# Hybrid trunk: attention with its tokens in their own order, V made with tokens stationary

## The chip, the cores and the metric

The kernel runs on one core of a Trainium2 chip. The core has a matrix engine (TensorE, "PE" in the profile, with its weight loads shown apart as "PEld"), a vector engine (VectorE, "DVE"), a scalar engine (ScalarE, "ACT"), a general engine (GpSimd, "POOL") and an engine that issues DMAs (SyncE, "SP"). Working memory is SBUF, 128 partitions wide; matrix products land in PSUM, which has eight banks of 512 fp32 values per partition. The metric is the device time of one execution in microseconds, the median of several runs.

## The reference

Two residual layers over 512 tokens of 1024 features, in fp32. Layer 0 mixes tokens by causal pooling, layer 1 by attention; each is followed by a SwiGLU, and a last norm ends it. The change lies in layer 1's attention. Its 16 heads of 64 features fall into three groups: 6 heads look at a window of 128 consecutive tokens, 5 at every fourth token (window 512, dilation 4), 5 at every sixteenth (window 2048, dilation 16). Here they are called near heads (0 to 5) and far heads (6 to 15).

```python
ATTN_PATTERNS = ((128, 1), (512, 4), (2048, 16))     # HEAD_GROUPS = (6, 5, 5)

def attn_mixer(h, w_qkv, w_out):
    qkv = jnp.einsum('bsd,de->bse', h, w_qkv).reshape(B, S, 3, N_HEADS, HEAD_DIM)
    q = rope(qkv[:, :, 0]) * HEAD_DIM ** -0.5
    k = rope(qkv[:, :, 1])
    v = qkv[:, :, 2]
    ...
    for (window, dilation), n_g in zip(ATTN_PATTERNS, HEAD_GROUPS):
        o_g, lse_g = dilated_window_attention(q[:, :, sl], k[:, :, sl], v[:, :, sl], window, dilation)
        outs.append(o_g)
        lses.append(jax.nn.logsumexp(lse_g, axis=-1) - math.log(n_g))
    alpha = jax.nn.softmax(jnp.stack(lses, axis=-1), axis=-1)
    merged = jnp.concatenate(
        [o_g * (N_ATTN_GROUPS * alpha[:, :, g]).astype(o_g.dtype)[:, :, None, None] for g, o_g in enumerate(outs)],
        axis=2,
    ).reshape(B, S, D_ATTN)
    return jnp.einsum('bse,ed->bsd', merged, w_out)
```

Within `dilated_window_attention` the tokens of one residue (position modulo the dilation) see only each other, causally, up to the window.

## The kernel before

**Products in three terms.** Every large fp32 product is made of three in a rounded format (fp32r): an operand is split into `hi`, a rounded copy (a ScalarE copy), and `lo`, the rest (a VectorE subtraction), and the products hi x hi, hi x lo and lo x hi are added up in PSUM. `split` does so for activations (L311 to L313), `weights` for weights (L137, L138).

**Weights.** `enqueue` lists all weight tiles in the order of use. `weights(i)` (L119) issues the DMAs of the next tiles on SP's queue into a ring of five raw tiles, splits the next few, and hands out tile i. All engines but PE get their order from a scheduler that works from priorities; `tc.high_priority(URGENT)` raises the priority of what stands in it. PE's order is that of the program (`manual_schedule`).

**The normed input.** `h_hi` and `h_lo` hold the normed activations with features on partitions, 8 chunks of 512 tokens. `turned` (L329) fills them: it transposes a block of 128 tokens by PE and splits the result into its places, which `in_order` (L315) or `by_residue` (L319) gives. For attention it is `by_residue`: position r * 128 + j holds token 4 j + r, so that the tokens of one residue modulo 4 are consecutive. The tables of cosines and sines stand in the same order (`TOKENS`, L53).

**Queries and keys.** For each pair of heads t = 0 to 7, `project` (L226) makes q and k as 24 matmuls (8 chunks x 3 terms) with a 128 x 128 weight stationary and 512 tokens moving, and `rope` (L816) turns them: a shuffle and two multiplications (one on GpSimd), then an addition that writes the result. Its addition (L824 to L830) writes far heads' q and k as they stand; near heads' q into token order, and near heads' k into an order by block of 128 tokens, and by residue within it. The masks of the near heads (`key` in `_constants`, L1138) follow that order. The first three products are made in two halves of tokens (`by_halves`), because the last block of tokens comes late.

**Steps.** A counter of steps runs through this: `later(step)` (L922) runs one head's transposes and one set of scores that are due. `near_scores` and `far_scores` make the scores on PE, mask them and take the maxima on VectorE, and take exponentials on ScalarE (`soften`); `transposes` turns the exponentials by PE into `pT` one step later. `between(step)` (L1032) also starts the sums of the groups' shares at step 19, the groups' weights at 21, and their spread over the features, with a transposition on PE, at 22.

**V.** `v` holds tokens on partitions, four blocks of 128, for all 1024 features. Near heads' 384 features (`VA`) are made as three products with weights stationary and 512 tokens moving, steps 16 to 18; ScalarE copies each out in blocks (L1057), and `turn` (L1044) transposes its four blocks by PE (L1048) and copies them to `v` (L1049). The far heads' 640 features are made in two parts of 320 (`VB`): tokens are stationary, 128 of one residue at a time, the weights' 320 columns move, and four PSUM banks hold the four blocks through 4 x 2 chunks of features (L1071 to L1073), in steps 19 to 26. At the last chunk each block's bank is copied to `v`, two by ScalarE (L1078) and two by VectorE (L1076).

**The merge.** For each pair of heads, products of `v` and `pT` (L1100 to L1104) go to one PSUM bank of the same ring of four, VectorE multiplies by the shares (L1108), and the result is split into `h_hi`, `h_lo` for the output projection.

Of the kernel before, what the change touches and what calls it, by code (L numbers as in the profile page):

```python
# [17 lines left out]
P = 128  # L18
S = 512
# [30 lines left out]
)  # L50

TWO = [(g, i) for g in (0, 1) for i in (0, 3)] + [(g, i) for i in (1, 2, 4, 5, 6) for g in (0, 1)]
TOKENS = np.arange(S).reshape(J, R).T.reshape(-1)  # L53
BY_GROUP = [6, 7, 4, 5, 2, 3, 0, 1]


# [1 line left out]
def trunk_kernel(ctx: ExitStack, tc: tile.TileContext, x_in, xT, gam, gains, consts, ident_d, w0, wT, w1, wv, w_down, out):  # L58
# [260 lines left out]
    def by_residue(b):  # L319

        n = P // R

        def places(h, half, tp):
            at = h[:, 4 * half : 4 * half + 4, :].rearrange("p c (r j) -> p c r j", r=R)
            return at[:, :, :, b * n : (b + 1) * n], tp.rearrange("p c (i r) -> p c r i", r=R)

        return places

    def turned(norm, shift, b, tps, order):  # L329

# [183 lines left out]
    def ffn(layer, norm, third, nxt):  # L514
# [8 lines left out]
        with ExitStack() as fctx:  # L523
# [267 lines left out]
    with ExitStack() as actx:  # L791
# [17 lines left out]
        ap.tile([P, 8], F32, name="gap3")  # L809
        state = {}  # L810

        def blocks_of(a):

            return a.rearrange("p (r b i) -> p b r i", r=R, b=4)

        def rope(ps, t, name):  # L816
            a = aw.tile([P, S], F32, name="ropea")
            sw = aw.tile([P, S], F32, name="ropeb")
            nc.vector.stream_shuffle(sw, ps, PARTNER)
            nc.vector.tensor_mul(a, ps, cosr)  # L820
            nc.gpsimd.tensor_mul(sw, sw, sinr)
            out = aw.tile([P, S], F32, name=name, bufs=3)

            if t >= 3:  # L824
                nc.vector.tensor_add(out, a, sw)
            elif name == "k":
                nc.vector.tensor_add(out.rearrange("p (b r i) -> p b r i", b=4, r=R), blocks_of(a), blocks_of(sw))
            else:
                by_r = lambda z: z.rearrange("p (r j) -> p r j", r=R)
                nc.vector.tensor_add(out.rearrange("p (j r) -> p r j", r=R), by_r(a), by_r(sw))  # L830
            return out

        def slot(h, i):
# [94 lines left out]
                pend_tr.extend((step + 1, *got) for got in run(*args))  # L928

        h_hi, h_lo = tokens_at(0)  # L930
        late = lambda b: turned(norm, 0, b, [ptr.tile([P, 4, P], F32, name="tp") for _ in range(2)], by_residue(b))

        def by_halves(js):

            n = J // 2
            part = lambda z, i: z.rearrange("p (r j) -> p r j", r=R)[:, :, i * n : (i + 1) * n]
            got = [(mm.tile([P, S], F32, name="mm"), weights(j, held=i)) for i, j in enumerate(js)]
            for i in range(2):
                for at, (ps, (whi, wlo)) in enumerate(got):
                    if i == 0 and at == 2:  # L940
                        late(3)
                    for c in range(NC):
                        mm3(part(ps, i), whi[:, c, :], wlo[:, c, :], part(h_hi[:, c, :], i), part(h_lo[:, c, :], i),
                            i + c == 0, c == NC - 1, skip_group_check=True)
            return [ps for ps, _ in got]

# [92 lines left out]
                spread_weights()  # L1039


        to_turn = []

        def turn():  # L1044
            m, vt = to_turn.pop(0)
            tp = ptr.tile([P, 4, P], F32, name="tp")
            for b in range(4):
                nc.tensor.transpose(tp[:, b, :], vt[:, b * P : (b + 1) * P], ident)  # L1048
            nc.scalar.copy(v[:, :, m * P : (m + 1) * P], tp)  # L1049

        step = 16
        for m in range(3):
            ps = project(j_v0[m], h_hi, h_lo)
            if to_turn:
                turn()
            vt = aw.tile([P, S], F32, name="ropea")
            nc.scalar.copy(vt.rearrange("p (b r i) -> p b r i", b=4, r=R), blocks_of(ps))  # L1057
            to_turn.append((m, vt))
            between(step)
            step += 1  # L1060
        for part in range(2):
            at = VA + part * VB
            pv = [mm.tile([P, S], F32, name="mm") for _ in range(4)]
            for c in range(4):
                whi, wlo = weights(j_v[part][c])
                for b in range(4):
                    for kk in range(2):
                        kc = 2 * c + kk
                        o = pv[b][:, :VB]
                        xh, xl = (z[:, kc, b * P : (b + 1) * P] for z in (h_hi, h_lo))  # L1070
                        nc.tensor.matmul(o, lhsT=xh, rhs=whi[:, kk, :], start=kc == 0, stop=False)  # L1071
                        nc.tensor.matmul(o, lhsT=xh, rhs=wlo[:, kk, :], start=False, stop=False)
                        nc.tensor.matmul(o, lhsT=xl, rhs=whi[:, kk, :], start=False, stop=kc == NC - 1)  # L1073
                    if c == 3:
                        if b // 2:
                            nc.vector.tensor_copy(v[:, b, at : at + VB], pv[b][:, :VB])  # L1076
                        else:
                            nc.scalar.copy(v[:, b, at : at + VB], pv[b][:, :VB])  # L1078
# [12 lines left out]
        for t in range(8):  # L1091
            ps = mm.tile([P, S], F32, name="mm")
            for h in (2 * t, 2 * t + 1):
                base = HD * (h % 2)
                rows = slice(base, base + HD)
                cols = slice(h * HD, (h + 1) * HD)
                for b in range(4):
                    o = ps[rows, b * P : (b + 1) * P]
                    if h >= 6:
                        nc.tensor.matmul(o, lhsT=v[:, b, cols], rhs=pT[:, slot(h, b), :], start=True, stop=True)  # L1100
                    else:
                        nc.tensor.matmul(o, lhsT=v[:, b, cols], rhs=pT[:, slot(h, 2 * b), :], start=True, stop=b == 0)
# [3 lines left out]
            by_r = lambda z: z.rearrange("p (r j) -> p r j", r=R)  # L1106
            in_turn = lambda z: z.rearrange("p (j r) -> p r j", r=R)
# [13 lines left out]
def _constants():  # L1121
# [12 lines left out]
    cos = np.tile(np.concatenate([cos, cos], 0)[ROPE_ORDER], (2, 1))[:, TOKENS]  # L1134
    sin = np.tile(np.concatenate([-sin, sin], 0)[ROPE_ORDER], (2, 1))[:, TOKENS]
    q = np.arange(P)[:, None]
    k = np.arange(P)[None, :]
    key = R * (k % 32) + k // 32  # L1138
    near = np.where(key <= q, 0.0, NEG)
    prev = np.where(key >= q, 0.0, NEG)  # L1140
    own = np.where(k <= q, 0.0, NEG)
    comb = np.where((k <= q) & (k % 4 == q % 4), 0.0, NEG)
    parts = bands + [cos, sin, near, prev, near, own, comb]
    return np.ascontiguousarray(np.concatenate(parts, 1).astype(np.float32))


def _tiles(w, n):

    k = w.shape[0] // P
    return w.reshape(k, P, n, P).transpose(2, 1, 0, 3).reshape(n, P, k * P)  # L1150


def _layout(x, norm_mix, norm_ffn, norm_final, pool_w_in, pool_w_group, pool_scale, pool_w_out,
# [9 lines left out]
    w0 = np.concatenate([w_in, grp, qk, _tiles(qkv[:, 2 * D :], 8)[:3]], 0)  # L1163
    gu = [np.stack([_tiles(ffn_w_gate[i], NF), _tiles(ffn_w_up[i], NF)], 1).reshape(2 * NF, P, 1024) for i in range(2)]
    wv = qkv[:, 2 * D :].reshape(NC, P, D).transpose(1, 0, 2)
    wv = np.concatenate([wv[:, :, a:b].reshape(P, -1) for a, b in ((VA, VA + VB), (VA + VB, D))], 1)
# [19 lines left out]
```

## Time and profile before

| what | value |
|---|---|
| median of 3 runs | 1008.01 us (1007.27 to 1009.94) |
| the profiled execution | 1007.57 us |
| its span, first to last instruction | 1005.8 us |
| mean granted TensorE clock | 0.998 |
| near V, weights stationary, and the last scores | 557.9 to about 577.8 us of the span |
| far V, tokens stationary | about 577.8 to 607.5 us |
| merge of heads | about 607.5 to 622 us |

In a row of the timeline, the first number is the start in us from the span's start, the second the duration of the group, then engine, source line, operation, the tiles written and read, and the shapes; "x4" is a count, and a bracket at the end tells how long the engine had been idle and what released it. In a row of a line (`L830 DVE ...`) stand count, then shortest, median and longest duration in ns. In a row of groups, the numbers behind the bar are busy us in total and mean ns of one, then the idle time of the engine before them. In the table of stretches each engine has its busy us with the number of instructions. Matmuls are pipelined: one's duration includes time in which the next already runs.

### The profile page before, as it was taken

To read this page: it belongs to the slowest core of one execution; us is meant where nothing else is said; L and a number is where in the kernel's file an instruction comes from. 1 tells how busy PE (TensorE), PEld (TensorE's weight loads), DVE (VectorE), ACT (ScalarE), POOL (GpSimd) and SP (SyncE) were. 2 spreads that over 40 slices of the span, in tenths; PEclk is the share of its full clock that TensorE was granted. 3 is DMA by queue.
4 is the path that set the end of the run, shared out by engine and by line. 5 is a ranking of instruction groups with operands and counts; after the bars stand their busy time and mean duration, and the time that the engine had idled before them with its cause. 6 is when DMAs were issued, how large, how long until landed. Compare 5 with 4: busy or idle time off the path is not lost.

```text
span 1005.8 us, 16546 instructions
## 1 busy us (share of the span) xinstructions
PE 994.0 (99%) x6559; PEld 906.4 (90%) x6559; DVE 784.4 (78%) x1117; ACT 528.7 (53%) x834; POOL 110.8 (11%) x110
## 2 busy tenths in 40 slices
PE   9999999999999999999999999999999999999997
PEld 7888999989989998988788898889998998999895
DVE  6484899898897888787887557479989889788875
ACT  5573666545544554572454444357654554555354
POOL 0002010111002010002112032101011110111000
PEclk9999999999999999999999999999999999999999
DMA  9457276678559765523221249426766855975512
GB/s 353 155 189 167 63 210 158 158 199 236 144 129 288 169 150 144 188 83 99 71 69 53 82 152 268 85 63 186 183 155 193 235 147 123 290 178 141 153 64 83
DMA packets 76189, 157.30 MB, mean 156 GB/s; under 512 B 5760, under 2 KB 5888, under 8 KB 76112
## 3 DMA queue, kind: packets, MB, share of 16 engines
q1 hardware_dynamic: 57856, 121.00, 35.7%
q0 software_dynamic: 17968, 34.99, 20.3%
q8 instruction: 51, 0.84, 0.3%
q14 instruction: 26, 0.21, 0.1%
q10 hardware_dynamic: 288, 0.27, 0.1%
HBM read 154.08 MB, written 2.13 MB: 155 GB/s over the span
## 4 chain that ended last, share of the span: by engine, by line
PE 94%; DVE 2%; DMA 1%; ACT 1%; issue 1%; ACTq 0%; DVEq 0%
PE p L602 25%; PE r L602 13%; PE r L685 10%; PE mm L602 6%; PE p L685 5%; PE mm L222 4%; PE mm L224 4%; PE mm L223 4%; PE mm L739 3%; PE mm L685 2%; PE mm L354 2%; PE mm L352 2%; PE mm L353 2%; DMA wraw<-wT 1%; PE early L223 1%; PE early L224 1%
## 5 line engine op out<-in xcount | busy, mean ns | idle before, releaser
L137 ACT CAST whi<-wraw 128x1024 fp32r<-128x1024 f32 (+2 forms) x190 | 185.4, 978 | 178.4 <-issue 34.4
L138 DVE TENSOR_TENSOR wlo<-wraw,whi 128x1024 fp32r<-128x1024 f32 (+2 forms) x190 | 220.4, 1160 | 74.9 <-ACT whi L137 74.1
L137 ACT CAST whi<-vraw 128x1024 fp32r<-128x1024 f32 (+1 forms) x102 | 99.6, 976 | 144.8 <-DVE vraw L140 54.0
L602 PE MATMUL p<-t_hi,wlo 128*128 128x256 f32 x528 | 149.8, 284 | 0.0
L602 PE MATMUL p<-t_lo,whi 128*128 128x256 f32 x528 | 149.5, 283 | 0.0
L602 PE MATMUL p<-t_hi,whi 128*128 128x256 f32 x528 | 148.4, 281 | 0.0
L138 DVE TENSOR_TENSOR wlo<-vraw,whi 128x1024 fp32r<-128x1024 f32 (+1 forms) x102 | 114.9, 1127 | 14.2 <-ACT whi L137 13.9
L602 PEld LDWEIGHTS p<-t_hi,whi 128*128 128x128 f32 x528 | 100.0, 189 | 0.0
L602 PE MATMUL r<-h_hi,wlo 128*128 128x256 f32 x352 | 99.9, 284 | 0.0
L602 PEld LDWEIGHTS p<-t_hi,wlo 128*128 128x128 f32 x528 | 99.6, 189 | 0.0
L602 PE MATMUL r<-h_lo,whi 128*128 128x256 f32 x352 | 99.6, 283 | 0.0
L602 PEld LDWEIGHTS p<-t_lo,whi 128*128 128x128 f32 x528 | 99.3, 188 | 0.0
L602 PE MATMUL r<-h_hi,whi 128*128 128x256 f32 x352 | 99.0, 281 | 0.0
L140 DVE TENSOR_TENSOR vraw<-vraw,wraw 128x1024 f32<-128x1024 f32 x68 | 76.6, 1127 | 0.8
L106 POOL DMA_DIRECT2D wraw<-w x22 | 26.6, 1211 | 428.0 <-DMA wraw<-w 171.2
L602 PEld LDWEIGHTS r<-h_hi,whi 128*128 128x128 f32 x352 | 66.7, 189 | 0.0
L602 PEld LDWEIGHTS r<-h_hi,wlo 128*128 128x128 f32 x352 | 66.4, 189 | 0.0
L602 PEld LDWEIGHTS r<-h_lo,whi 128*128 128x128 f32 x352 | 66.2, 188 | 0.0
L222 PE MATMUL mm<-h_hi,whi 128*128 128x512 f32 (+1 forms) x176 | 65.2, 370 | 0.0
L224 PE MATMUL mm<-h_hi,wlo 128*128 128x512 f32 (+1 forms) x176 | 63.6, 361 | 0.0
L223 PE MATMUL mm<-h_lo,whi 128*128 128x512 f32 (+1 forms) x176 | 63.5, 361 | 0.0
L685 PE MATMUL r<-whi,u_lo 128*128 128x512 f32 x144 | 56.1, 390 | 0.0
(315 smaller groups left out, 2489.9 us busy)
## 6 DMA issues: line engine op xcount, KB each, us to landing
wraw<-w SPq DMA_DIRECT2D x116, 512.0 KB, 4.8
wraw<-w_down SPq DMA_DIRECT2D x32, 512.0 KB, 3.6
vraw<-w SPq DMA_DIRECT2D x22, 512.0 KB, 5.2
wraw<-w POOLq DMA_DIRECT2D x22, 512.0 KB, 7.6
vraw<-w POOLq DMA_DIRECT2D x22, 512.0 KB, 8.4
wraw<-wT SPq DMA_DIRECT2D x16, 512.0 KB, 4.7
wraw<-w_down SPq DMA_DIRECT2D x24, 256.0 KB, 2.7
vraw<-w_down SPq DMA_DIRECT2D x6, 512.0 KB, 5.3
```

Source lines behind the costliest of these rows:

```text
L106: nc.gpsimd.dma_start(dst, more, accum_op=ALU.add)
L137: nc.scalar.copy(hi[:, :n], raw[:, :n])
L138: nc.vector.tensor_sub(lo[:, :n], raw[:, :n], hi[:, :n].bitcast(F32))
L140: nc.vector.tensor_add(raws[into][:, :n], raws[into][:, :n], raws[more][:, :n])
L222: nc.tensor.matmul(ps, lhsT=whi, rhs=xhi, start=first, stop=False, **kw)
L223: nc.tensor.matmul(ps, lhsT=whi, rhs=xlo, start=False, stop=False, **kw)
L224: nc.tensor.matmul(ps, lhsT=wlo, rhs=xhi, start=False, stop=last, **kw)
L352: nc.tensor.matmul(ps, lhsT=xhi, rhs=w[0][:, k, :], start=first, stop=False)
L353: nc.tensor.matmul(ps, lhsT=xhi, rhs=w[1][:, k, :], start=False, stop=False)
L602: nc.tensor.matmul(ps[:, g, :], lhsT=w[:, g, c, :], rhs=xx[:, c, :], start=i in (0, 1, 3) and g + c + k == 0, stop=c == 3 and k == 2, skip ...
L685: nc.tensor.matmul(acc[t], lhsT=u, rhs=w, start=i in (0, 1, 3) and c + k == 0, stop=c == len(pairs) - 1 and k == 2, skip_group_check=True,)
L739: nc.tensor.matmul(ps, lhsT=u, rhs=w[:, m, :], start=z + m + k == 0, stop=z == 1 and m == 1 and k == 2,)
```

## The change

The normed input of attention stays in token order, and so do the tables of angles. Near heads' q and k are written as they stand; far heads' q and k are written by residue by the addition in `rope`, which reads its two operands at a step of four tokens. All of V is made with tokens stationary, in three parts of 384, 320 and 320 features: in the first a block is 128 consecutive tokens, in the others it is every fourth token of the 512, so that the weight load of the far parts reads the tokens of `h_hi` and `h_lo` at a step of four. The products of near V with weights stationary, their copies and transposes go. The evictions of all parts stand in `tc.high_priority(URGENT)`. There are 12 steps of V instead of 11, four for each part; the step numbers in `between` stay. Near masks become plain causal ones.

```diff
-VA = 6 * HD
-VB = 5 * HD
+V_PARTS = ((0, 6 * HD), (6 * HD, 5 * HD), (11 * HD, 5 * HD))
...
-    j_v0 = [enqueue(w0[26 + i], (8, P)) for i in range(3)]
-    j_v = []
-    for at in (0, VB):
-        j_v.append([enqueue(wv[:, 8 * at + c * 2 * VB : 8 * at + (c + 1) * 2 * VB], (2, VB)) for c in range(4)])
+    j_v = [[enqueue(wv[:, 8 * at + c * 2 * n : 8 * at + (c + 1) * 2 * n], (2, n)) for c in range(4)] for at, n in V_PARTS]
...
-            turn_block = lambda b: turned(norm, 0, b, [r_tile() for _ in range(2)], by_residue(b))
+            turn_block = lambda b: turned(norm, 0, b, [r_tile() for _ in range(2)], in_order(b))
...
+        by_r = lambda z: z.rearrange("p (r j) -> p r j", r=R)
+        in_turn = lambda z: z.rearrange("p (j r) -> p r j", r=R)
...
-            if t >= 3:
+            if t < 3:
                 nc.vector.tensor_add(out, a, sw)
-            elif name == "k":
-                nc.vector.tensor_add(out.rearrange("p (b r i) -> p b r i", b=4, r=R), blocks_of(a), blocks_of(sw))
             else:
-                by_r = lambda z: z.rearrange("p (r j) -> p r j", r=R)
-                nc.vector.tensor_add(out.rearrange("p (j r) -> p r j", r=R), by_r(a), by_r(sw))
+                nc.vector.tensor_add(by_r(out), in_turn(a), in_turn(sw))
...
-        late = lambda b: turned(norm, 0, b, [ptr.tile([P, 4, P], F32, name="tp") for _ in range(2)], by_residue(b))
+        late = lambda b: turned(norm, 0, b, [ptr.tile([P, 4, P], F32, name="tp") for _ in range(2)], in_order(b))
...
-                        mm3(part(ps, i), whi[:, c, :], wlo[:, c, :], part(h_hi[:, c, :], i), part(h_lo[:, c, :], i),
+                        mm3(ps[:, HALVES[i]], whi[:, c, :], wlo[:, c, :], h_hi[:, c, HALVES[i]], h_lo[:, c, HALVES[i]],
...
-        to_turn = []
-
-        def turn():
...
         step = 16
-        for m in range(3):
-            ps = project(j_v0[m], h_hi, h_lo)
-            if to_turn:
-                turn()
-            vt = aw.tile([P, S], F32, name="ropea")
-            nc.scalar.copy(vt.rearrange("p (b r i) -> p b r i", b=4, r=R), blocks_of(ps))
-            to_turn.append((m, vt))
-            between(step)
-            step += 1
-        for part in range(2):
-            at = VA + part * VB
+        for part, (at, n) in enumerate(V_PARTS):
+            tokens = lambda z, b: z[:, b * P : (b + 1) * P] if part == 0 else in_turn(z)[:, b, :]
             pv = [mm.tile([P, S], F32, name="mm") for _ in range(4)]
             for c in range(4):
                 whi, wlo = weights(j_v[part][c])
                 for b in range(4):
                     for kk in range(2):
                         kc = 2 * c + kk
-                        o = pv[b][:, :VB]
-                        xh, xl = (z[:, kc, b * P : (b + 1) * P] for z in (h_hi, h_lo))
+                        o = pv[b][:, :n]
+                        xh, xl = (tokens(z[:, kc, :], b) for z in (h_hi, h_lo))
                         nc.tensor.matmul(o, lhsT=xh, rhs=whi[:, kk, :], start=kc == 0, stop=False)
                         nc.tensor.matmul(o, lhsT=xh, rhs=wlo[:, kk, :], start=False, stop=False)
                         nc.tensor.matmul(o, lhsT=xl, rhs=whi[:, kk, :], start=False, stop=kc == NC - 1)
                     if c == 3:
-                        if b // 2:
-                            nc.vector.tensor_copy(v[:, b, at : at + VB], pv[b][:, :VB])
-                        else:
-                            nc.scalar.copy(v[:, b, at : at + VB], pv[b][:, :VB])
-                if to_turn:
-                    turn()
+                        with tc.high_priority(URGENT):
+                            if b // 2:
+                                nc.vector.tensor_copy(v[:, b, at : at + n], pv[b][:, :n])
+                            else:
+                                nc.scalar.copy(v[:, b, at : at + n], pv[b][:, :n])
                 between(step)
                 step += 1
...
-    key = R * (k % 32) + k // 32
-    near = np.where(key <= q, 0.0, NEG)
-    prev = np.where(key >= q, 0.0, NEG)
     own = np.where(k <= q, 0.0, NEG)
+    prev = np.where(k >= q, 0.0, NEG)
     comb = np.where((k <= q) & (k % 4 == q % 4), 0.0, NEG)
-    parts = bands + [cos, sin, near, prev, near, own, comb]
+    parts = bands + [cos, sin, own, prev, own, own, comb]
```

More of the change, by code (lines that the diff above doesn't have):

```diff
@@ L52 @@
 TWO = [(g, i) for g in (0, 1) for i in (0, 3)] + [(g, i) for i in (1, 2, 4, 5, 6) for g in (0, 1)]
-TOKENS = np.arange(S).reshape(J, R).T.reshape(-1)
 BY_GROUP = [6, 7, 4, 5, 2, 3, 0, 1]
@@ L317, in in_order @@
         return lambda h, half, tp: (h[:, 4 * half : 4 * half + 4, b * P : (b + 1) * P], tp)
[L319 to L327, printed above, removed]
     def turned(norm, shift, b, tps, order):
@@ L810, in trunk_kernel @@
         state = {}
-        def blocks_of(a):
-            return a.rearrange("p (r b i) -> p b r i", r=R, b=4)
+        by_r = lambda z: z.rearrange("p (r j) -> p r j", r=R)
+        in_turn = lambda z: z.rearrange("p (j r) -> p r j", r=R)
         def rope(ps, t, name):
@@ L930, in trunk_kernel @@
         h_hi, h_lo = tokens_at(0)
-        late = lambda b: turned(norm, 0, b, [ptr.tile([P, 4, P], F32, name="tp") for _ in range(2)], by_residue(b))
+        late = lambda b: turned(norm, 0, b, [ptr.tile([P, 4, P], F32, name="tp") for _ in range(2)], in_order(b))
         def by_halves(js):
-            n = J // 2
-            part = lambda z, i: z.rearrange("p (r j) -> p r j", r=R)[:, :, i * n : (i + 1) * n]
             got = [(mm.tile([P, S], F32, name="mm"), weights(j, held=i)) for i, j in enumerate(js)]
@@ L1039, in between @@
                 spread_weights()
-        to_turn = []
-        def turn():
[L1045 to L1049, printed above, removed]
-        step = 16
-        for m in range(3):
-            ps = project(j_v0[m], h_hi, h_lo)
-            if to_turn:
-                turn()
-            vt = aw.tile([P, S], F32, name="ropea")
-            nc.scalar.copy(vt.rearrange("p (b r i) -> p b r i", b=4, r=R), blocks_of(ps))
-            to_turn.append((m, vt))
-            between(step)
-            step += 1
-        for part in range(2):
-            at = VA + part * VB
+        step = 16
+        for part, (at, n) in enumerate(V_PARTS):
+            tokens = lambda z, b: z[:, b * P : (b + 1) * P] if part == 0 else in_turn(z)[:, b, :]
             pv = [mm.tile([P, S], F32, name="mm") for _ in range(4)]
@@ L1133, in _constants @@
     sin = np.sin(ang.astype(np.float64))
-    cos = np.tile(np.concatenate([cos, cos], 0)[ROPE_ORDER], (2, 1))[:, TOKENS]
-    sin = np.tile(np.concatenate([-sin, sin], 0)[ROPE_ORDER], (2, 1))[:, TOKENS]
+    cos = np.tile(np.concatenate([cos, cos], 0)[ROPE_ORDER], (2, 1))
+    sin = np.tile(np.concatenate([-sin, sin], 0)[ROPE_ORDER], (2, 1))
     q = np.arange(P)[:, None]
     k = np.arange(P)[None, :]
-    key = R * (k % 32) + k // 32
-    near = np.where(key <= q, 0.0, NEG)
-    prev = np.where(key >= q, 0.0, NEG)
     own = np.where(k <= q, 0.0, NEG)
+    prev = np.where(k >= q, 0.0, NEG)
     comb = np.where((k <= q) & (k % 4 == q % 4), 0.0, NEG)
-    parts = bands + [cos, sin, near, prev, near, own, comb]
+    parts = bands + [cos, sin, own, prev, own, own, comb]
     return np.ascontiguousarray(np.concatenate(parts, 1).astype(np.float32))
@@ L1162, in _layout @@
     qk = np.stack([_tiles(rot(qkv[:, :D]), 8), _tiles(rot(qkv[:, D : 2 * D]), 8)], 1).reshape(16, P, 1024)
-    w0 = np.concatenate([w_in, grp, qk, _tiles(qkv[:, 2 * D :], 8)[:3]], 0)
+    w0 = np.concatenate([w_in, grp, qk], 0)
     gu = [np.stack([_tiles(ffn_w_gate[i], NF), _tiles(ffn_w_up[i], NF)], 1).reshape(2 * NF, P, 1024) for i in range(2)]
     wv = qkv[:, 2 * D :].reshape(NC, P, D).transpose(1, 0, 2)
-    wv = np.concatenate([wv[:, :, a:b].reshape(P, -1) for a, b in ((VA, VA + VB), (VA + VB, D))], 1)
+    wv = np.concatenate([wv[:, :, at : at + n].reshape(P, -1) for at, n in V_PARTS], 1)
     return dict(
```

2 lines of the change are left out of this document (removed).

## The prediction

> **What bounds the kernel now.** I read the page first: the line of engines and the chain that ended last.
>
> ```profile
> span 1005.8 us, 16546 instructions
> PE 994.0 (99%) x6559; PEld 906.4 (90%) x6559; DVE 784.4 (78%) x1117; ACT 528.7 (53%) x834; POOL 110.8 (11%) x110
> PE 94%; DVE 2%; DMA 1%; ACT 1%; issue 1%; ACTq 0%; DVEq 0%
> ```
>
> TensorE works through the whole span and carries 94% of the chain. So a change counts by the matmul time it adds or takes away, and by the few places where PE waits. Next the table of stretches (queries and keys; the last of these with the first V step; the rest of V; the merge of heads) and the waits of PE.
>
> ```profile
> core 0: us, PE busy (x) PEld busy (x) DVE busy (x) ACT busy (x) POOL busy (x), PEclk, DMA share, GB/s
> 495.70:557.90 62.20, 62.20 (x346) 50.58 (x344) 48.68 (x94) 28.66 (x96) 11.22 (x10) 1.00 0.19 58
> 557.90:577.80 19.90, 19.90 (x109) 16.53 (x108) 9.95 (x19) 10.04 (x40) 0.79 (x1) 1.00 0.30 86
> 577.80:607.50 29.70, 29.70 (x208) 29.56 (x206) 15.59 (x38) 13.19 (x21) 8.00 (x15) 1.00 0.56 162
> ...
> PE mm L1102 <- ACT v L1078: 1.4, 1, 1.4
> PE tp L913 <- ACT e L841: 0.7, 2, 0.5
> ```
>
> In the V stage PE is never idle, VectorE and ScalarE only half the time busy, and the clock is full. In the far part (577.80 to 607.50) the weight loads are as busy as the matmuls. Attention's only waits of note are 1.4 us for a copy of V out of PSUM and 0.7 us for exponentials.
>
> Busy times of matmuls overlap, so I price them by pace: start to start, from the timeline.
>
> ```profile
> 558.75 0.39 PE L222 MATMUL mm<-h_hi,whi 128*128 128x512 f32 x1
> 562.84 0.39 PE L222 MATMUL mm<-h_hi,whi 128*128 128x512 f32 x1
> ...
> 569.43 0.60 PE L1048 MATMUL tp<-ident,ropea 128*128 128x128 f32 x4
> 569.86 0.60 PE L913 MATMUL tp<-ident,e 128*128 128x128 f32 x4
> ...
> 587.16 0.31 PE L1071 MATMUL mm<-whi,h_hi 128*128 128x320 f32 x1
> 590.68 0.31 PE L1071 MATMUL mm<-whi,h_hi 128*128 128x320 f32 x1
> ...
> 616.89 5.15 PE L1100 MATMUL mm<-pT,v 128*64 128x128 f32 x77
> ```
>
> From 558.75 to 562.84 lie 18 matmuls of 512 columns, 227 ns each. From 587.16 to 590.68 lie 24 of 320 columns, 147 ns each. The difference over 192 columns gives 0.42 ns a column. Four transposes take 0.43 us, 108 ns each. They move only 128 columns; the L1100 rows move as many but load 64 columns instead of 128, and start every 64 ns (4.88 us over 76). So 108 ns is the pace of a 128-column load, and a 320-column matmul hides it with 39 ns to spare.
>
> **The change, part by part.** *Near V.* Out go 3 x 24 = 72 matmuls of 512 columns (72 x 227 = 16.34 us) and 3 x 4 = 12 transposes (3 x 0.43 = 1.30 us). In come 4 x 4 x 2 x 3 = 96 matmuls of 384 columns. These aren't in the trace; between 320 and 512 the pace is 147 + 64 x 0.42 = 174 ns (147 and 227 bound it), 16.67 us in all. Tokens are consecutive there, so their loads stay at 108 ns. Near V: +0.33 - 1.30 = -0.97 us. The ScalarE copies that go with it were off the path, and four evictions of 384 columns replace six copies of 512, in a stage where that engine is half idle. Three weight splits of 1024 become four of 768: the same elements, hidden by the same idle time. One more load is issued on SP's queue, for the same bytes.
>
> *Far V.* The 192 matmuls of 320 columns stay, but each now loads its 128 tokens at a step of four fp32, 16 bytes. No stationary or moving operand of before has a step within a row, so I bound the load. The nearest rows are VectorE's.
>
> ```profile
> L830 DVE TENSOR_TENSOR q<-ropea,ropeb x3: 1069/1101/1105, 463.7 to 481.5; 128x512 f32<-128x512 f32 x3
> L825 DVE TENSOR_TENSOR q<-ropea,ropeb x5: 691/692/693, 496.2 to 552.8; 128x512 f32<-128x512 f32 x5
> L977 DVE TENSOR_TENSOR mx<-mx,gsums x2: 180/180/180, 549.9 to 574.4; 128x20 f32<-128x20 f32 x2
> L977 DVE TENSOR_TENSOR mx<-mx,near x1: 205/205/205, 516.0 to 516.0; 128x24 f32<-128x24 f32 x1
> L313 DVE TENSOR_TENSOR u_lo<-ct,u_hi 128x1280 fp32r<-128x1280 f32 x16 | 23.8, 1490 | 2.0 <-ACT u_hi L312 2.0
> L313 DVE TENSOR_TENSOR u_lo<-ct,u_hi 128x512 fp32r<-128x512 f32 x24 | 16.4, 685 | 2.1 <-ACT u_hi L312 2.1
> ```
>
> L830 and L825 are the same addition; L830 writes at a step of 16 bytes and takes 1092 ns on the mean (its group in the list of lines would read the same) instead of 692: 0.78 ns more an element. L313 at two sizes gives the plain price, (1490 - 685) / 768 = 1.05 ns. So VectorE pays 1.83 ns for an element that lies 16 bytes from the last. Reads do the same: L977 reads `near` at a step of 32 bytes and needs 25 ns more for 4 more elements, some 21 ns more than plain for 24. And PE's own moving operand crosses 16 bytes (four columns) in 4 x 0.42 = 1.68 ns. Nothing in this trace crosses 16-byte steps faster than that; the new load at full pace would have to, one every 0.84 ns.
>
> Lower bound: no cost, the load stays under 147 ns (a gain is excluded, since the 320 moving columns set that pace). Upper bound: VectorE's 1.83 ns, 128 x 1.83 = 234 ns a load, 192 x (234 - 147) = 16.7 us. I take the row nearest in engine, PE's own 1.68 ns: 215 ns a load, now longer than the matmul, so it sets the pace: 192 x (215 - 147) = **13.1 us**. Nothing hides it, because every matmul has a load of its own.
>
> [...]
>
> *Rotary additions.* Three q additions fall from 1.09 to 0.69 us, ten (q and k of the far heads) now read at a step of four and by L977 may rise to 1.1. One of the three is on a chain on which PE waits:
>
> ```profile
> 481.47 1.07 DVE q L830
> 482.54 1.11 DVE e L869 x2
> 483.65 1.19 DVE mx L873 x2
> 484.95 1.98 ACT e L841 x8
> ```
>
> The scores' masking waits in VectorE's queue behind that addition and PE's transposes wait for the exponentials, so 0.40 us comes off the 0.7 us wait: -0.40 us (bounds 0 and -0.7). The ten longer ones, +4.1 us at most, lie in 495.70 to 557.90, where VectorE idles 13.5 us and PE doesn't wait. Were that cover gone, the exponentials would be late and each addition would cost 0.4 us. The writes of h change from a step of four in the PSUM read to plain:
>
> ```profile
> L312 ACT CAST h_hi<-r 128x512 fp32r<-128x512 f32 x6 | 3.5, 579 | 1.6 <-PE r L309 1.6
> L312 ACT CAST h_hi<-sc 128x512 fp32r<-128x512 f32 x4 | 2.3, 582 | 3.1 <-PE sc L309 3.1
> ```
>
> 579 ns by residue, 582 ns in order: nothing.
>
> *Evictions with priority.* The timeline of ScalarE and PE at the end of V:
>
> ```profile
> 605.20 1.05 ACT L137 CAST bhi<-wraw 128x1024 fp32r<-128x1024 f32 x1 [3.26 <-DMA wraw<-wT]
> 607.10 0.42 ACT L1078 COPY v<-mm 128x320 f32<-128x320 f32 x1
> 610.50 1.04 ACT L137 CAST bhi<-wraw 128x1024 fp32r<-128x1024 f32 x1 [2.98 <-DMA wraw<-wT]
> 611.45 0.42 ACT L1078 COPY v<-mm 128x320 f32<-128x320 f32 x1
> 611.92 0.65 PE L1102 MATMUL mm<-pT,v 128*64 128x128 f32 x4 [1.43 <-ACT v L1078]
> ```
>
> The second copy stands behind a cast that waits 2.98 us for its DMA, and the merge of the second pair of heads needs the bank it frees. Placed first, it costs PE nothing: -1.43 us (bounds 0, if the order stays, and -1.43). What is late next is the product with `far` weights on VectorE (L1108), which must free banks for pairs 4 to 7; at worst it takes 1.0 us back. There are now three boundaries of four banks instead of two; at each the first eviction has the 18 matmuls of the other three blocks as cover (18 x 174 = 3.1 us after the near part, 18 x 147 = 2.6 us after a far one). Behind it in ScalarE's queue stand casts for later steps, for which nobody waits.
>
> *Order of steps.* There are 12 steps instead of 11 and group sums, weights and spread stay at 19, 21 and 22, so they come sooner in PE's order.
>
> ```profile
> 570.39 1.16 PE L884 MATMUL sc<-k,q 64*128 64x128 f32 x16
> 586.58 0.35 DVE L1011 TENSOR_TENSOR den<-den,gw 128x24 f32<-128x24 f32 x3
> 593.32 0.27 PE L1020 MATMUL tp<-ident,den 128*64 128x128 f32 x1
> ```
>
> From the last scores to `den` takes 16.5 us. Before the last scores lie two chunks of 24 matmuls of 174 instead of 227 ns and one V transposition less: they move by 2 x 24 x 0.053 + 0.43 = 3.0 us to 567.4, so `den` is there at 584. Before PE's transposition of it lie four near and three far chunks (16.7 + 10.6 us) instead of three and four (16.3 + 14.1) and 1.3 us of transposes: it moves from 593.3 to about 589. That leaves 5 us: no cost.
>
> The sum: -0.97 - 0.40 - 1.43 + 13.1 = **+10.3 us**. On the profiled execution's 1007.57 us that is 1017.9. The median shown is 1008.01, 0.4 above, so I say **1018.0 us**.
>
> **Rivals.** *The strided load stays hidden (not slower).* The load keeps its 108 ns, or anything to 147, if PE's load path takes one fp32 each 0.84 ns wherever it lies. For it: each load has a whole matmul's time and 39 ns to spare, and PE's load is another path than its moving operand or VectorE. Against it: the rows above. Then the sum is -2.8 us, 1004.8, to 1005.8 if the merge takes 1.0 back. It decides by one point: a load of less than 147 ns. [...]
>
> *The load slows in proportion to its own clock*, as VectorE's element did: 1.83 / 1.05 x 108 = 188 ns. Then 192 x 41 = 7.9 us, in all +5.1: 1012.7.
>
> *The priority doesn't do what it says, or evictions find a new wait at the two inner boundaries*: 1.43 us stays, or is paid twice more. With a free load 1006.2 to 1009.1; with a slow one it's covered.
>
> **How the numbers follow.** Chances: load bound by 16-byte steps (1018, to 1021.5 at the upper price) 0.42; load hidden 0.38; in proportion 0.12; evictions at fault with a hidden load 0.08. About 0.3%, 3.0 us, is what a measurement of this kernel can tell from no change, so the line on the fast side is 1005.0. The hidden case lies across it: 0.18 faster, 0.20 the same. The eviction case is nearly all the same: 0.06, with 0.02 slower. Slower: 0.42 + 0.12 + 0.02 = 0.56; same 0.26; faster 0.18. Both signs hold much of the chance, so the range takes both cases in, 1004.3 to 1021.5; the likeliest case's own is 1015 to 1021.5.
>
> **What would show it.** In the timeline of the changed kernel: far V matmuls starting every 215 ns (188, or 147 if I am wrong), near ones every 174; no transposes of `ropea`; no 1.43 us wait before the second pair; q additions of the near heads at 0.69 us and the ten of the far ones near 1.1. What would make the prediction wrong is above all a pace of 147 ns in far V.

## The result and the profile after

The change makes the kernel slower: 1023.32 us, the median of 4 runs (1021.95 to 1024.51), against 1008.42 for the kernel before (4 runs). The ratio is 1.0144, with a 95% interval of 1.0131 to 1.0158. The prediction was 1018.0, in a range of 1004.3 to 1021.5 that held both signs: the sign and the cause of its likeliest case were right, the size too small.

The page of the kernel after, its line of engines and its chain (the profiled execution took 1024.01 us):

```profile
span 1022.2 us, 16574 instructions
PE 1012.3 (99%) x6571; PEld 926.5 (91%) x6571; DVE 789.0 (77%) x1120; ACT 527.2 (52%) x831; POOL 110.8 (11%) x110
PE 94%; DVE 3%; ACT 1%; issue 1%; DMA 0%; POOL 0%; ACTq 0%; POOLq 0%
```

PE still fills the span and the chain as before, and has only 12 matmuls more. Weight loads are busy 20.1 us longer. So either the matmuls themselves became slower, or PE idles between them in gaps too short for the list of waits. The waits of PE, after (us in total, times, longest):

```profile
PE mm L251 <- DVE odd_rows L245: 1.1, 1, 1.1
PE tp L893 <- ACT e L821: 0.4, 2, 0.2
PE r L304 <- ACT ct L298: 0.3, 1, 0.3
```

Both of attention's waits went the predicted way: the 1.4 us for V's eviction is gone and the 0.7 us for exponentials is 0.4. The loss shows in PE's timeline (start, duration, line), first two rows of the near part, then three of the far part:

```profile
561.25 0.34 PE L1031 MATMUL mm<-whi,h_hi 128*128 128x384 f32 x1
...
564.39 0.33 PE L1031 MATMUL mm<-whi,h_hi 128*128 128x384 f32 x1
...
608.47 0.39 PE L1031 MATMUL mm<-whi,h_hi 128*128 128x320 f32 x1
...
610.57 0.39 PE L1031 MATMUL mm<-whi,h_hi 128*128 128x320 f32 x1
...
612.67 0.40 PE L1031 MATMUL mm<-whi,h_hi 128*128 128x320 f32 x1
```

Between the two near rows lie 18 matmuls, 174 ns each. Between neighbours of the far rows lie 9, 2.10 us, so 233 ns each, where before it was 147. The narrower matmul is now the slower one. The rows of weight loads (count; shortest, median, longest in ns) say why; first after, where near and far share a line, then before, far only:

```profile
L1031 PEld LDWEIGHTS mm<-whi,h_hi x96: 186/329/331, 560.6 to 625.1; 128*128 128x128 f32 x96
```

```profile
L1071 PEld LDWEIGHTS mm<-whi,h_hi x64: 187/188/190, 577.8 to 606.9; 128*128 128x128 f32 x64
```

A load at consecutive tokens is recorded at 186 ns, one at a step of four at 329. A recorded load, like a matmul, includes time in which it overlaps its neighbours (187 to 190 ns at a pace of 147 before), so the prices below come from starts.

The table splits the span at PE's own events (starts of the matmuls that are named, in us; the last row runs to the end of the span). The last two columns are experiments, told below.

| stage | before | after | e1_plain | e9_behind_all |
|---|---|---|---|---|
| start to layer 0's first SwiGLU product | 114.48 | 116.67 | 116.23 | 114.68 |
| to attention's first scores | 357.17 | 357.18 | 357.21 | 357.15 |
| to the last near scores | 38.64 | 38.70 | 38.75 | 38.63 |
| to the last scores | 60.99 | 58.40 | 58.39 | 60.99 |
| to the merge's first product | 36.32 | 55.11 | 40.85 | 36.32 |
| merge, first to last product | 14.17 | 12.15 | 12.15 | 13.24 |
| to the end of the span | 384.00 | 384.00 | 383.99 | 384.04 |

V is in the fourth and fifth rows: together 97.31 before, 113.51 after, +16.20 us. The merge gives 2.02 back. The first row's +2.19 isn't the change's: edits of either kernel ran with and without it (last section). From the first SwiGLU product on, the change costs 905.53 - 891.29 = 14.24 us.

### The profile page after: what moved, and what is told of

Same layout as the page of the kernel before. It is cut to its first block, busy times and chain, and to the rows that moved or that the text cites. A ratio compares the mean times of both kernels' runs of the same rounds, so it can differ in the third digit from the quotient of the medians.

```text
span 1022.2 us, 16574 instructions
## 1 busy us (share of the span) xinstructions
PE 1012.3 (99%) x6571; PEld 926.5 (91%) x6571; DVE 789.0 (77%) x1120; ACT 527.2 (52%) x831; POOL 110.8 (11%) x110
## 4 chain that ended last, share of the span: by engine, by line
PE 94%; DVE 3%; ACT 1%; issue 1%; DMA 0%; POOL 0%; ACTq 0%; POOLq 0%
PE p L587 25%; PE r L587 12%; PE r L670 10%; PE mm L587 6%; PE p L670 5%; PE mm L217 3%; PE mm L219 3%; PE mm L218 3%; PE mm L724 3%; PE mm L670 2%; PE mm L339 2%; PE mm L337 2%; PE mm L338 2%; PE mm L1031 2%; PE mm L1033 2%; PE mm L1032 2%
## 5 line engine op out<-in xcount | busy, mean ns | idle before, releaser
L136 DVE TENSOR_TENSOR wlo<-wraw,whi 128x1024 fp32r<-128x1024 f32 (+3 forms) x191 | 220.8, 1156 | 87.2 <-ACT whi L135 86.5
L135 ACT CAST whi<-wraw 128x1024 fp32r<-128x1024 f32 (+3 forms) x191 | 185.8, 974 | 196.1 <-issue 39.4
L670 PE MATMUL r<-wlo,u_hi 128*128 128x512 f32 x144 | 56.2, 390 | 0.0
L670 PE MATMUL r<-whi,u_hi 128*128 128x512 f32 x144 | 56.1, 389 | 0.0
L217 PE MATMUL mm<-h_hi,whi 128*128 128x512 f32 (+1 forms) x152 | 55.6, 366 | 0.0
```

The costliest lines, as they stand in the source:

```text
L135: nc.scalar.copy(hi[:, :n], raw[:, :n])
L136: nc.vector.tensor_sub(lo[:, :n], raw[:, :n], hi[:, :n].bitcast(F32))
L217: nc.tensor.matmul(ps, lhsT=whi, rhs=xhi, start=first, stop=False, **kw)
L670: nc.tensor.matmul(acc[t], lhsT=u, rhs=w, start=i in (0, 1, 3) and c + k == 0, stop=c == len(pairs) - 1 and k == 2, skip_group_check=True,)
```

## The experiments

The theory: a weight load pays about 1.8 ns (233 / 128) for each 16-byte line it touches, and when that is longer than the matmul it sets the pace. A line is here 16 consecutive bytes of a partition, four tokens of a chunk, as a unit for counting; no run shows how the memory itself is divided. Rivals: any step makes a load slow; the load slows with the distance of elements in some other way; the loss is due to the later order of work around V; the wait that went away was removed by the priority, or by something else.

**e1_plain: far part without the step.** In the kernel after, the far parts load consecutive tokens like the near part.

```diff
-            tokens = lambda z, b: z[:, b * P : (b + 1) * P] if part == 0 else in_turn(z)[:, b, :]
+            tokens = lambda z, b: z[:, b * P : (b + 1) * P]
```

> The changed kernel, with 128 consecutive tokens stationary in the far parts too (the far heads' V then holds other tokens than the reference's; nothing else differs). Theory A, the load of a stationary operand at a 16-byte step sets the pace: the far matmuls go back from 233 to 147 ns, 192 x 86 ns = 16.5 us off, about 1006.5 us, a little under the kernel before. Theory B, the new steps, evictions or their order cost the time and the step of the load is incidental: the pace stays above 200 ns and the time above 1018 us.

Measured: 1009.22 us, ratio to before 1.0003 (0.9993 to 1.0013). Weight loads and the far pace in e1_plain:

```profile
L1031 PEld LDWEIGHTS mm<-whi,h_hi x96: 186/188/190, 560.2 to 608.3; 128*128 128x128 f32 x96
```

```profile
600.04 0.31 PE L1031 MATMUL mm<-whi,h_hi 128*128 128x320 f32 x1
...
603.56 0.31 PE L1031 MATMUL mm<-whi,h_hi 128*128 128x320 f32 x1
```

24 matmuls in 3.52 us: 147 ns again. From the first SwiGLU product to the end e1_plain takes 891.34 us where after takes 905.53. So the step is the 14.2 us, and no order of work is: 16.6 us of slower pace (192 x 86.4 ns) less a wait of PE that the slow part hides. Without the step that wait comes back, so there is no gain either. PE's waits, ScalarE's timeline and PE's timeline of e1_plain at the end of V:

```profile
PE mm L1061 <- ACT v L1039: 2.4, 1, 2.4
```

```profile
607.94 2.16 ACT L135 CAST bhi<-wraw 128x1024 fp32r<-128x1024 f32 x2 [1.40 <-DMA wraw<-wT]
610.01 1.04 ACT L135 CAST whi<-wraw 128x1024 fp32r<-128x1024 f32 x1
610.96 0.75 ACT L1039 COPY v<-mm 128x320 f32<-128x320 f32 x2
```

```profile
608.70 0.31 PE L1033 MATMUL mm<-whi,h_lo 128*128 128x320 f32 x1
611.43 0.65 PE L1061 MATMUL mm<-pT,v 128*64 128x128 f32 x4 [2.42 <-ACT v L1039]
```

The copies of V have raised priority here, and still stand behind three casts of 1024 columns, the first of which waited 1.40 us for its DMA.

**e2_step2, e3_step3: a smaller step.** The far parts load tokens at a step of two (8 bytes) or three (12 bytes), so 128 tokens touch 64 or 96 lines of 16 bytes instead of 128.

```diff
-            tokens = lambda z, b: z[:, b * P : (b + 1) * P] if part == 0 else in_turn(z)[:, b, :]
+            tokens = lambda z, b: z[:, b * P : (b + 1) * P] if part == 0 else z.rearrange("p (h j r) -> p h r j", h=2, r=2)[:, b // 2, b % 2, :]
...
+            tokens = lambda z, b: z[:, b * P : (b + 1) * P] if part == 0 else z[:, : 3 * P].rearrange("p (j r) -> p r j", r=3)[:, b % 3, :]
```

> The changed kernel with the far parts' tokens at a step of two fp32, 8 bytes (the far heads' V then holds other tokens than the reference's). Law 1, a load costs 1.82 ns for each 16 bytes it crosses and nothing for a second element in them: 128 elements cross 64 such steps, 116 ns, hidden, pace 147 ns, about 1006.5 us. Law 2, an element in new 16 bytes costs 1.82 ns and one in the same 16 bytes 0.84: 64 x 1.82 + 64 x 0.84 = 170 ns, pace 170, about 1011 us. Law 3, any step but one costs the full price: 233 ns, about 1023 us.

> The changed kernel with the far parts' tokens at a step of three fp32, 12 bytes (the far heads' V then holds other tokens than the reference's). Law 1: 96 crossings x 1.82 = 175 ns, pace 175, about 1012 us. Law 2: 96 x 1.82 + 32 x 0.84 = 202 ns, about 1017 us. Law 3: 233 ns, about 1023 us.

Measured: 1008.14 and 1010.83 us, one run each, so the paces are what counts. Loads and far pace in the lines and the timeline of e2_step2, then of e3_step3:

```profile
L1031 PEld LDWEIGHTS mm<-whi,h_hi x96: 186/195/197, 558.6 to 606.7; 128*128 128x128 f32 x96
...
590.13 0.31 PE L1031 MATMUL mm<-whi,h_hi 128*128 128x320 f32 x1
...
594.52 0.31 PE L1031 MATMUL mm<-whi,h_hi 128*128 128x320 f32 x1
```

```profile
L1031 PEld LDWEIGHTS mm<-whi,h_hi x96: 186/261/268, 558.6 to 612.1; 128*128 128x128 f32 x96
...
592.32 0.34 PE L1031 MATMUL mm<-whi,h_hi 128*128 128x320 f32 x1
...
594.96 0.34 PE L1031 MATMUL mm<-whi,h_hi 128*128 128x320 f32 x1
```

At 8 bytes 30 matmuls take 4.39 us, 146 ns: the recorded load is 7 ns longer and the pace unchanged. At 12 bytes 15 take 2.64 us, 176 ns: the load now bounds. 176 / 96 = 1.83 ns a line, and 233 / 128 = 1.82 ns: one price fits both. At 8 bytes it gives 64 x 1.82 = 117 ns, an estimate, which the matmul's 147 would hide; the pace of 146 agrees. "Any step is slow" falls with e2_step2. One reading stays open beside the lines: at these three steps the lines touched (64, 96, 128) and the bytes crossed (1024, 1536, 2048) grow alike, so a price for each 16 bytes crossed fits as well. Only a step beyond 16 bytes would part the two, and no run has one for a load.

**e4_near_step4: the step in the near part too.**

```diff
-            tokens = lambda z, b: z[:, b * P : (b + 1) * P] if part == 0 else in_turn(z)[:, b, :]
+            tokens = lambda z, b: in_turn(z)[:, b, :]
```

> The changed kernel with the near part's tokens at a step of four as well (the near heads' V then holds other tokens than the reference's). If the load bounds the pace and lies beside the matmul before it, the 96 matmuls of 384 columns start every 233 ns like those of 320, 96 x 59 ns = 5.7 us more, about 1029 us. If the step is paid on top of the matmul (320 columns: 147 + 86), it is 174 + 86 = 260 ns, 8.3 us more, about 1031.5 us.

Measured: 1027.85 us, one run. The near part in its timeline:

```profile
560.15 0.40 PE L1031 MATMUL mm<-whi,h_hi 128*128 128x384 f32 x1
...
563.65 0.40 PE L1031 MATMUL mm<-whi,h_hi 128*128 128x384 f32 x1
```

15 matmuls in 3.50 us: 233 ns for 384 columns, the same as for 320. The moving columns no longer matter at this step: the 86 ns that the step adds to a matmul of 320 columns aren't paid on top of the 174 of one of 384. The load runs beside the matmul, and here it is the longer. Behind the first SwiGLU product e4_near_step4 takes 911.43 us, 5.90 more than after; 96 x (233 - 174) is 5.7.

**e5_before_priority, e6_after_no_priority: the priority alone.** e5 raises the priority of V's copies in the kernel before (those of the far part); e6 takes it away in the kernel after, for all three parts. The edit of e5:

```diff
-                        if b // 2:
-                            nc.vector.tensor_copy(v[:, b, at : at + VB], pv[b][:, :VB])
-                        else:
-                            nc.scalar.copy(v[:, b, at : at + VB], pv[b][:, :VB])
+                        with tc.high_priority(URGENT):
+                            if b // 2:
+                                nc.vector.tensor_copy(v[:, b, at : at + VB], pv[b][:, :VB])
+                            else:
+                                nc.scalar.copy(v[:, b, at : at + VB], pv[b][:, :VB])
```

> The kernel before with nothing changed but the priority of the evictions of far V. If the wait of 1.43 us before the second pair of heads comes from the eviction standing behind a cast that waits for its DMA, PE no longer waits there and 1.4 to 2.0 us go: 1006 to 1006.6 us against 1008.0. If the scheduler's order stays or VectorE's products give the time back later in the merge: 1008.

> The changed kernel without the priority. If the slow far part gives the weights' DMAs time to land, no eviction stands behind a waiting cast and the time stays at 1022 to 1023.5 us. If the wait returns, at the last or at an inner boundary, 1.4 us or more come on top: over 1024.5 us.

Measured: e5 1009.73 us, ratio to before 1.0000 (0.9989 to 1.0012); e6 1023.55 us, ratio to before 1.0140 (1.0121 to 1.0159), with the same stages as after (V's two rows 113.49, merge 12.15). PE's waits and ScalarE's timeline of e5:

```profile
PE mm L1103 <- ACT v L1079: 2.2, 2, 1.9
```

```profile
607.71 1.05 ACT L137 CAST bhi<-wraw 128x1024 fp32r<-128x1024 f32 x1 [3.76 <-DMA wraw<-wT]
608.66 1.05 ACT L137 CAST whi<-wraw 128x1024 fp32r<-128x1024 f32 x1
609.61 0.41 ACT L1079 COPY v<-mm 128x320 f32<-128x320 f32 x1
613.41 1.04 ACT L137 CAST bhi<-wraw 128x1024 fp32r<-128x1024 f32 x1 [3.39 <-DMA wraw<-wT]
614.36 0.42 ACT L1079 COPY v<-mm 128x320 f32<-128x320 f32 x1
```

With priority the second copy still comes behind a cast that waits 3.39 us for a DMA, in the order of the kernel before, and the waits for V's copies come to 2.2 us instead of 1.4. And without it, the kernel after has no such wait. So the priority gains nothing here (why it leaves the order as it is, no run shows); what frees PE in the kernel after is the slow far part itself. ScalarE's timeline of the kernel after at the same place:

```profile
615.92 1.99 ACT L135 CAST bhi<-wraw 128x1024 fp32r<-128x1024 f32 x2
620.57 1.05 ACT L135 CAST whi<-wraw 128x1024 fp32r<-128x1024 f32 x1 [2.66 <-PE mm L1033]
621.97 0.43 ACT L1039 COPY v<-mm 128x320 f32<-128x320 f32 x1 [0.35 <-PE mm L1033]
623.37 0.42 ACT L1039 COPY v<-mm 128x320 f32<-128x320 f32 x1 [0.97 <-PE mm L1033]
```

In these rows ScalarE waits for PE, not for a DMA (its one such wait in the far parts, 1.6 us, ends at 612.08, well before these copies): with the far part 16 us longer the weights have landed in time. e3_step3 says the same from the other side. Its far part should cost 192 x (176 - 147) = 5.6 us over e1_plain and costs 894.41 - 891.34 = 3.1, because its list of waits has no wait for V's copies, which is worth 2.4 in e1_plain.

**e7_rope_plain: far additions without the step.** In the kernel after, far heads' q and k are added and written in token order, so that far scores are taken between tokens in another order.

```diff
-                nc.vector.tensor_add(by_r(out), in_turn(a), in_turn(sw))
+                nc.vector.tensor_add(out, a, sw)
```

> The changed kernel with the far heads' rotary additions reading and writing plainly (their q and k then stand in token order, and their scores are those of other tokens than the reference's). If the additions that read at a step of four delay the near heads' exponentials behind them in VectorE's queue, the additions fall from 1.08 to 0.69 us, PE's waits for exponentials at the transposes of the second and third near pair vanish, and first scores to first far scores shortens by about 0.7 us. If those waits have another cause, they stay.

Measured: 1021.13 us, one run. The additions in the kernel after (near heads L808, far heads L810):

```profile
L808 DVE TENSOR_TENSOR q<-ropea,ropeb x3: 679/679/681, 465.9 to 483.7; 128x512 f32<-128x512 f32 x3
L810 DVE TENSOR_TENSOR q<-ropea,ropeb x5: 1072/1085/1103, 498.1 to 555.5; 128x512 f32<-128x512 f32 x5
L810 DVE TENSOR_TENSOR k<-ropea,ropeb x5: 1058/1077/1094, 505.6 to 562.0; 128x512 f32<-128x512 f32 x5
```

and in e7, with the two groups of near transposes behind the first two far additions in PE's timeline of e7, then of the kernel after:

```profile
L810 DVE TENSOR_TENSOR q<-ropea,ropeb x5: 693/693/693, 496.1 to 552.7; 128x512 f32<-128x512 f32 x5
...
501.17 1.01 PE L893 MATMUL tp<-ident,e 128*128 128x128 f32 x7
516.05 1.07 PE L893 MATMUL tp<-ident,e 128*128 128x128 f32 x7
```

```profile
503.17 1.41 PE L893 MATMUL tp<-ident,e 128*128 128x128 f32 x7
518.44 1.47 PE L893 MATMUL tp<-ident,e 128*128 128x128 f32 x7
```

Seven transposes take 0.40 us longer twice: PE idles inside the group, too briefly for the list of waits. The list's own 0.4 us for exponentials stands at 487 us after, ahead of every far addition, and is the same in e7. The stages agree: to the last near scores e7 takes 38.31 us (after 38.70), to the last scores 57.99 (58.40), 0.80 in all. The two are the first q additions of the far heads. They stand in VectorE's queue ahead of the masking (L849) of the near scores behind those transposes, as in its timeline of the kernel after:

```profile
498.06 1.08 DVE L810 TENSOR_TENSOR q<-ropea,ropeb 128x512 f32<-128x512 f32 x1 [0.28 <-POOL ropeb L805]
...
499.54 1.28 DVE L849 SCALAR_TENSOR_TENSOR e<-sc,gain 128x512 f32<-128x512 f32 x2
```

The other eight cost PE nothing: the later stages are the same in both.

**e8_behind_some, e9_behind_all: what the change wanted, done otherwise.** On the kernel before, the weights of the output projection are ordered behind V's last copy by an explicit edge, which priority couldn't do. e9 does so for all of them, e8 only for those from its fourth step on.

```diff
-                            nc.scalar.copy(v[:, b, at : at + VB], pv[b][:, :VB])
+                            evicted = nc.scalar.copy(v[:, b, at : at + VB], pv[b][:, :VB])
...
-            w = weights(js[i])
+            with behind():
+                w = weights(js[i])
...
-        ws = [weights(js[4 + i], split_ahead=4 + i, load_ahead=6 + i) for i in range(4)]
+        with behind():
+            ws = [weights(js[4 + i], split_ahead=4 + i, load_ahead=6 + i) for i in range(4)]
...
-        third = out_projection(j_wo, range(NC), m_hi, m_lo, norm, SHIFT, four, lambda: [sc_tile(), sc_tile()])
+        third = out_projection(j_wo, range(NC), m_hi, m_lo, norm, SHIFT, four, lambda: [sc_tile(), sc_tile()],
+                               behind=lambda: tc.issue_after(evicted.ins))
```

> The kernel before, with the casts of the last two of the four late output-projection tiles (bhi) and what is split with them queued behind the second eviction on ScalarE by an explicit edge, in place of a priority. If the eviction's wait is the order of ScalarE's queue, which a priority didn't change because those casts look ready earlier, PE no longer waits between the end of V and the second pair of heads: the merge takes 12.2 us instead of 14.2, about 2 us less from the first FFN matmul to the end. If the casts come too late for VectorE's products instead, PE waits at pairs 4 to 7 and nothing is won.

> The same with all four late tiles and the splits made with them queued behind the second eviction. The eviction's wait goes as in the other; but four more subtractions of 1.2 us then stand on VectorE among the products of the merge, which free PE's banks for pairs 4 to 7. If VectorE has room, 2 us less as there; if it hasn't, up to 3 us of new waits in the merge, and the time is that of before or 1 us more.

Measured: e8 1007.88 us, ratio to before 0.9993 (0.9983 to 1.0002). Its wait for V's copies is gone, but 1.4 us of waits for VectorE's product of the merge (L1110) stand in its place, and its merge takes 14.77 us where 12.2 was hoped for. e9 1006.83 us, ratio 0.9983 (0.9975 to 0.9992): the fastest kernel of this study. PE's waits and ScalarE's timeline of e9:

```profile
PE mm L1102 <- DVE o L1110: 0.5, 1, 0.5
```

```profile
605.24 0.43 ACT L1080 COPY v<-mm 128x320 f32<-128x320 f32 x1 [3.30 <-PE mm L1075]
606.12 0.43 ACT L1080 COPY v<-mm 128x320 f32<-128x320 f32 x1 [0.45 <-PE mm L1075]
606.45 1.05 ACT L137 CAST whi<-wraw 128x1024 fp32r<-128x1024 f32 x1
607.39 3.88 ACT L137 CAST bhi<-wraw 128x1024 fp32r<-128x1024 f32 x4
```

Both copies now come before the casts, and the merge falls from 14.17 to 13.24 us; 0.5 us of it is a wait for VectorE. The gain is best read from the stages: 891.29 - 890.38 = 0.9 us behind the first SwiGLU product, half of the 2 us hoped for. The medians differ by more (1008.47 of 21 runs before), probably because most of e9's 11 runs had the early start of the last section: ten of them lie between 1006.66 and 1007.21, but only the profiled one shows its start.

## Why the prediction fell short, by its steps

- **The load sets the pace: right.** So were the place (far V only) and the reason (16-byte steps). Hidden load (147 ns) and load in proportion (188 ns) are refuted by 233. With 0.42 for this case and 0.38 for the hidden load, the prediction had hardly chosen between them.
- **The price of the load: too low, and this is the step that failed**: "I take the row nearest in engine, PE's own 1.68 ns: 215 ns a load". It measured 233 ns, so the term of 13.1 us is 192 x (233 - 147) = 16.5, the upper bound (16.7) from VectorE's 1.83 ns. That 215 came as near as it did is luck. The row nearest in engine wasn't nearest in kind: a moving operand reads all four values of a line (4 x 0.42 = 1.68 ns), while VectorE's L830 touches one value a line (1.83 ns), as the load does (1.82 ns).
- **Near V: right.** 174 ns as interpolated. Taking the far part's 16.6 us (192 x 86.4 ns) and 0.41 us for the second far addition out of V's +16.20 leaves -0.8 us, where -0.97 was predicted.
- **Near q addition: nearly right.** 0.68 us instead of 1.10, and the wait for exponentials fell from 0.7 to 0.4 us; -0.40 was predicted. The stage to the last near scores agrees: 38.64 before, 38.31 in e7, where the far additions cost nothing.
- **Ten far additions where "PE doesn't wait": wrong for two of them.** They measured 1.08 us as bounded, but the cover, 13.5 us of idle time in the stretch, says nothing of the two that stand ahead of the masking on which PE's transposes hang. The prediction had their price in that case, 0.4 us each: 0.80 us by e7.
- **Evictions "Placed first": right sum, wrong cause, so luck.** The 1.43 us went, but for the reason that the far part became slow. In the rivals stood "with a slow one it's covered", and that is what happened; with a fast far part the wait returns at 2.4 us in spite of the priority. So the case of the hidden load would have been no change (e1_plain), not 2.8 us faster.
- **The merge** lost 2.02 us, 0.6 more than the one wait that was counted, and all of it lies at that wait. To the 25th product both merges take 2.29 us, to the 33rd 4.81 before and 2.78 after; between the 28th and the 29th lie 1.70 us before. The list's 1.43 counts only from the end of the row before, and rows of 0.27 us overlap at a pace of 0.06 to 0.11, so the entry was too small a price for the wait.
- **Order of steps: no cost**, as predicted; no wait for `den` or its spread appears.
- **The range.** With the upper price the predicted sum is 1007.57 + 10.3 + 3.4 = 1021.3. The profiled execution, without the late start, took 1024.01 - 2.19 = 1021.8, and the 0.80 of far additions less the merge's 0.6 make up nearly half of the rest. So the price alone didn't put the time outside the range. The sum was made on an execution with an early start, the profiled one after has the late one, and the range had no term for it: the kernel before alone runs from 1007.08 to 1010.66 in 21 runs. Which start the other three runs after had, nothing shows.

## What to carry to other kernels

Before a stationary operand is read at a step of up to 16 bytes, count the 16-byte lines that a load touches and compare lines x 1.82 ns, the price found here at 12 and 16 bytes, with the pace of the matmul that it stands beside: two fp32 to a line were free beside 320 columns (146 ns), one to a line cost 86 ns a matmul (233). Of two rows for an unseen price, take the one with the same access pattern rather than the same engine: here 1.83 ns came nearer to the load's 1.82 than 1.68 did. When copies wait behind casts that wait for DMAs, look whether a priority moves them at all; here only an explicit order did.

## What the runs showed of the hardware

**One price on two engines.** VectorE's stepped write cost 1.83 ns an element in the kernel before (worked out from L830, L825 and L313), PE's load 1.82 to 1.83 ns a line: nearly the same figure on engines with different plain prices (1.05 ns an element; a hidden load). That they share a cause isn't shown.

**Two starts.** PE's timelines at the start of the span, before and after, the same matmuls of 512 columns:

```profile
7.12 0.40 PE L222 MATMUL early<-whi,h_hi 128*128 128x512 f32 x1
...
9.17 0.39 PE L222 MATMUL early<-whi,h_hi 128*128 128x512 f32 x1
```

```profile
7.00 0.63 PE L217 MATMUL early<-whi,h_hi 128*128 128x512 f32 x1
...
9.56 0.63 PE L217 MATMUL early<-whi,h_hi 128*128 128x512 f32 x1
```

Before, 9 matmuls take 2.05 us, 228 ns each; after, 6 take 2.56 us, 427 ns each. It isn't the change: of the eleven kernels' profiled executions five had this start (the kernel after, e1, e5, e6, e8), and reached the first SwiGLU product about 2 us later (116.2 to 116.7 against 114.5 to 114.7). e5 and e8 are edits of the kernel before, and among the six with the early start are e2, e3, e4 and e7, edits of the kernel after. The granted clock in the table of stretches reads 1.00 for the first 10 us of both, but it counts as 1.00 whatever the trace's record of the clock leaves out. That record begins at 4.63 us of the span before and at 10.41 us after, and there the pace of after changes: its matmul at 10.41 us is followed by one at 10.65 and one at 10.88. In e1_plain and e6, which have the late start too, the starts of these matmuls go from 0.41 to 0.43 us apart to about 0.23 at 9.5 us; in the six traces with the early start they are 0.22 to 0.24 us apart from 6.4 us on. What decides between the two starts wasn't tried.
